# One plain chunk fewer ahead of the seven-product chunks, and one weight split held back in the queue

## The chip, the cores and the metric

The kernel runs on one core of one Trainium2 chip. The metric is device time in microseconds (us) for one execution, the median of the runs shown. Engines: PE is TensorE's matmul, PEld its weight load, DVE is VectorE, ACT is ScalarE, POOL is GpSimd, and SP is SyncE, whose queue (SPq) issues the loads. "L462" is line 462 of the kernel before.

## What is computed

A decoder trunk of two layers on 512 tokens of width 1024. Each layer is a SwiGLU feed-forward, a mixer, and a second feed-forward. All four feed-forwards have the same form, and the change touches only them:

```
h = h + 0.5 * swiglu(rmsnorm(h, g), wg, wu, wd)
def swiglu(u, wg, wu, wd):
    return (jax.nn.silu(u @ wg) * (u @ wu)) @ wd      # wg, wu: 1024 x 2816, wd: 2816 x 1024
```

The mixer of the first layer is a causal pooling, that of the second an attention over a shared latent. The final step is an RMSNorm.

## The kernel before

**Tiles and precision.** The 2816 hidden channels are 22 chunks of 128, and the model width is 8 chunks of 128; activations are held channel by token, 128 x 512. Every operand is split in two parts, hi and lo, and each product is three matmuls (`mm3`, L116 to L118): hi*hi, hi of the weights by lo of the data, lo of the weights by hi of the data. A weight unit of 128x1024 is loaded (tile `wraw`, 4 buffers), cast by ScalarE (`whi`) and its remainder taken by VectorE (`wlo`); plain units and the two wide units of a seven-product chunk share 4 buffers (`wsplit`).

**The plain chunks.** A feed-forward begins with chunks 0 and 1 (gate and up of both in four PSUM tiles, by `wfirst`), then chunk 2 (gate over all 8 channels, then up), then chunk 3 (gate and up in turn for each channel): 48 matmuls of 512 columns for a chunk. Behind the first channel of chunk 2's up part the norm's factor is spread over the partitions by two matmuls (`on_all`, L301 and L305, from `norm.spread`); its copy `rb` (ACT L307) is what every gate is multiplied by. `gated(g)` (L526 to L534) makes the middle values of a plain chunk: gate times rb (L530), silu (ACT L516), times rb again (L517), times up (L533), then cast and remainder (`split_mid`, L523 and L524: tiles `mh`, `ml`).

**The seven-product chunks.** From chunk `N_FIRST` = 4 on, gate and up of a chunk are made by a Strassen-like scheme of seven products P1 to P7 on 256 columns, of 12 matmuls each (84 for a chunk). `group_weights(g)` (L191) loads two raw units `ra` and `rb`, splits `a` (a11 and a12, for P1 and P2) and `f` (a22, for P4), has GpSimd make four sums in place (L201), and splits the sums: `s13` (for P5 and P7) behind the first two sums, `s24` (for P6 and P3) behind all four. The data side needs differences of halves: t1, t2 and t4 are made ahead, T3 (`prepare_t3`, L428 to L432 with L437) is written over the second half of the first four channels' operand, so only once the plain chunks have read it; P7 reads it. PSUM results are combined by way of copies: `c1` behind P1, `c16` behind P6, `c167` behind P7 (all ACT L462). P7 adds on to the tile that `c16` was copied from, so it waits for that copy. P4 and P3 of a chunk run during the next chunk; P3 is followed by L504, L478, silu, L517, L509, L510, `mh` and `ml`.

**Down products.** They are spread over the chunks by `down_steps(g)`: in chunk 4 the channels 0 and 1 take the middle values of chunks 0 and 1 (behind P2) and of chunk 2 (behind P5); in chunk 5, behind P2, they take those of chunk 3.

**What sets the order.** In the feed-forward PE runs in the order written. On ACT, DVE, POOL and SP a planner picks, when an engine comes free in its own model of the times, the first instruction in program order that is ready; that order is then fixed, and each engine runs it in turn. `queued_behind(steps)` adds an edge in the queue of the engine of each step, without a wait for the step's end. In the kernel before, the weights of chunk 4 and all T3 work are queued behind the last DVE step of the spread and behind the copy `rb`.

Of the kernel before, what the change touches and what calls it, by code (L numbers as in the profile page):

```python
# [16 lines left out]
P = 128  # L17
T = 512
D = 1024
ND = D // P  # L20
F = 2816
NF = F // P
HT = T // 2
N_FIRST = 4
PART = 4
N_MID = 8
H = 16
# [15 lines left out]
def down_steps(g):  # L43


    i, base = g % PART, g - g % PART - PART
    most, end, whole = range(base, base + PART - 1), [base + PART - 1], range(base, base + PART)
    if i == 0 and base == 0:
        return ([(d, most[:2], True, False) for d in range(2)], [(d, most[2:], False, False) for d in range(2)], [])
    if i == 0:  # L50
        return [], [], [(d, most, True, False) for d in range(2)]
    early = [(d, end, False, True) for d in range(2)] if i == 1 else []
    return early, [], [(d, whole, True, True) for d in (2 * i, 2 * i + 1)]
# [15 lines left out]
def trunk_kernel(  # L69
# [23 lines left out]
    nc = tc.nc  # L93
# [14 lines left out]
    def mm_tile():  # L108
        return psum.tile([P, T], F32, tag="mm", name="mm")
# [4 lines left out]
    def mm3(out, w, x, start, stop, **kw):  # L114

        nc.tensor.matmul(out, w[0], x[0], start=start, stop=False, **kw)  # L116
        nc.tensor.matmul(out, w[0], x[1], start=False, stop=False, **kw)  # L117
        nc.tensor.matmul(out, w[1], x[0], start=False, stop=stop, **kw)  # L118
# [67 lines left out]
    def split_into(tiles, raw, s):  # L186
        hi, lo = tiles
        nc.scalar.copy(hi[:, s], raw[:, s])  # L188
        nc.vector.tensor_tensor(out=lo[:, s], in0=raw[:, s], in1=f(hi[:, s]), op=ALU.subtract)  # L189

    def group_weights(idx, g, wb):  # L191

        ra, rb = (wraw_sb.tile([P, UNIT], F32, tag="wraw", name="wraw") for _ in range(2))
        nc.sync.dma_start(ra, wgu[idx, g - 2, 0])
        nc.sync.dma_start(rb, wgu[idx, g - 2, 1])
        q0, q1, whole = slice(0, 512), slice(512, UNIT), slice(0, UNIT)

        def add(out, x, y):  # L200
            nc.gpsimd.tensor_tensor(out=out, in0=x, in1=y, op=ALU.add)  # L201

        a = split_w(ra, wsplit_sb, "w")
        split_into(a, ra, whole)
        a22 = split_w(rb[:, q0], room.wf, "f")
        split_into(a22, rb[:, q0], q0)
        add(rb[:, q0], rb[:, q0], rb[:, q1])
        add(rb[:, q1], rb[:, q1], ra[:, q0])
        s13 = split_w(rb, wsplit_sb, "w")
        split_into(s13, rb, whole)  # L210
        add(ra[:, q0], rb[:, q0], ra[:, q0])
        add(ra[:, q1], ra[:, q0], ra[:, q1])
        s24 = split_w(ra, wb, "w")
        split_into(s24, ra, whole)
        a, a22, s13, s24 = part(a, 8, P), part(a22, 4, P), part(s13, 8, P), part(s24, 8, P)

        def of(w, at):
            return lambda k: [x[:, at + k] for x in w]

        return dict(a11=of(a, 0), a12=of(a, 4), a22=of(a22, 0), s1=of(s13, 0), s3=of(s13, 4), s2=of(s24, 0), s4=of(s24, 4))  # L220
# [227 lines left out]
    def ffn(idx, norm, on_h, first=None, last=None):  # L448
        with tc.tile_pool(name="mid", bufs=1) as midp, tc.tile_pool(name="wb", bufs=2) as wb, \
                tc.manual_schedule(engines={mybir.EngineType.PE}):  # L450
            weights, acc, act, mids = {}, {}, {}, {}

            def product(g, to, w, x, start=True):
                if start:
# [4 lines left out]

            def copy_of(g, name):  # L460
                t = act[g][name] = room.act.tile([P, HT], F32, tag=name, name=name)
                nc.scalar.copy(t, acc[g]["x"])  # L462
                return t

            def p1(g):
                product(g, "x", "a11", "b11")
# [70 lines left out]
            whole = slice(0, T)  # L537
# [29 lines left out]
                        norm.quarters.prepare(u)  # L567
            quarters, r, steps = norm.quarters, norm.r(), []
            ws = [part(load_w(wgu[idx, 0, m]), ND, P) for m in range(2)]
            for m in range(2):  # L570
                o = mm_tile()
                for c in range(ND):
                    mm3(o, [x[:, (c + 4 * m) % ND] for x in ws[m]], norm.gh[c], c == 0, c == ND - 1)
                    if m == 1 and c == 0:
                        rb = norm.spread(r, steps)
                        for j in range(2):
                            gated(j, ps[2 * j], ps[2 * j + 1])
                ps.append(o)
            gated(2, ps[4], ps[5])

            ws = [part(load_w(wgu[idx, 1, m]), ND, P) for m in range(2)]
            units[0] = part(load_w(wd[idx, 0]), 8, P)

            with queued_behind(steps):
                weights[N_FIRST] = group_weights(idx, N_FIRST, wb)
            ps = [mm_tile() for _ in range(2)]
            for c in range(ND):
                for m in range(2):
                    mm3(ps[m], [x[:, (c + 4 * m) % ND] for x in ws[m]], norm.gh[c], c == 0, c == ND - 1)
                if c == ND // 2 - 1:  # L590
                    with queued_behind(steps):
                        for k in range(ND // 2):
                            quarters.prepare_t3(k)
            gated(3, *ps)

            before = None
            for g in range(N_FIRST, NF):
                early, middle, late = down_steps(g)
                if g > N_FIRST:
                    weights[g] = group_weights(idx, g, wb)  # L600
                acc[g], act[g] = {}, {}
                p1(g)
                p2(g)
# [538 lines left out]
```

## Time and profile before

| | |
|---|---|
| time, median of 2 runs | 1725.56 us (1724.69 to 1726.42) |
| the profiled execution | 1728.71 us, its span 1726.9 us |
| PE busy | 1706.3 us, 99% of the span, 10816 matmuls |
| PEld, DVE, ACT, POOL busy | 1543.4, 1302.8, 850.9, 570.0 us (89, 75, 49, 33%) |
| granted TensorE clock, mean of the span | 0.995 |
| DMA | 166.77 MB, 31% of the 16 engines' time |

A busy PE is not PE at its peak, because matmuls overlap; the distance from one start to the next says more than a duration. Feed-forwards 1 to 4 have their chunk 2 at about 32, 406, 770 and 1386 us of the span.

### The profile page before, as it was taken

What the parts mean: (1) busy time and instruction counts of PE and PEld (TensorE: products, weight loads), DVE (VectorE), ACT (ScalarE), POOL (GpSimd) and SP (SyncE); (2) the same over time, 40 slices, a digit from 0 to 9 for tenths busy, and PEclk for the clock granted to TensorE, in tenths of its full rate; (3) what the DMA queues carried; (4) which work ended last, traced back from release to release, by engine and by line L of the source; (5) the groups of instructions that cost most, each with busy time, mean ns of one, the idle gap of its engine ahead of it and who ended that gap; (6) DMA issues with size and microseconds to landing.
All of it is one profiled execution on the core that took longest, in us unless ns stands there. A gap on an engine that the chain in (4) does not pass through costs nothing. (4 is left out here: it accounts for less than half of the span.)

```text
span 1726.9 us, 27436 instructions
## 1 busy us (share of the span) xinstructions
PE 1706.3 (99%) x10816; PEld 1543.4 (89%) x10816; DVE 1302.8 (75%) x2086; ACT 850.9 (49%) x1391; POOL 570.0 (33%) x388
## 2 busy tenths in 40 slices
PE   8999999999999999999999999999999999999998
PEld 6899999998899999888999999888888889999997
DVE  8877777789777777897777777787765787777775
ACT  6544444464444444454444444586655544444443
POOL 2433344133333344113334432422221234334421
PEclk9999999999999999999999999999999999999999
DMA  6233333322333322332333333332231232333331
GB/s 208 86 99 110 110 91 95 121 87 62 110 99 110 109 91 95 106 95 86 111 111 92 94 108 104 94 90 56 61 86 62 72 100 86 111 110 98 95 102 50
DMA packets 49585, 166.77 MB, mean 97 GB/s; under 512 B 6320, under 2 KB 6320, under 8 KB 49456
## 3 DMA queue, kind: packets, MB, share of 16 engines
q1 hardware_dynamic: 49312, 164.98, 31.1%
q8 instruction: 85, 1.39, 0.3%
q14 instruction: 44, 0.36, 0.1%
q10 hardware_dynamic: 144, 0.04, 0.0%
HBM read 158.44 MB, written 2.10 MB: 93 GB/s over the span
## 5 line engine op out<-in xcount | busy, mean ns | idle before, releaser
L201 POOL TENSOR_TENSOR wraw<-wraw 128x512 f32<-128x512 f32 x288 | 438.9, 1525 | 749.2 <-DVE flo L189 703.5
L116 PE MATMUL mm<-gh_hi,whi 128*128 128x256 f32 (+1 forms) x1424 | 435.2, 306 | 6.9 <-ACT c L462 6.9
L118 PE MATMUL mm<-gh_hi,wlo 128*128 128x256 f32 (+1 forms) x1424 | 435.1, 306 | 1.1 <-DVE wlo L146 1.1
L117 PE MATMUL mm<-gh_lo,whi 128*128 128x256 f32 (+1 forms) x1424 | 434.7, 305 | 0.5 <-DVE gh_lo L328 0.5
L188 ACT CAST whi<-wraw 128x1024 fp32r<-128x1024 f32 x216 | 226.9, 1053 | 207.7 <-POOL wraw L201 184.4
L116 PEld LDWEIGHTS mm<-gh_hi,whi 128*128 128x128 f32 x1424 | 274.6, 193 | 21.6 <-ACT c L462 8.6
L117 PEld LDWEIGHTS mm<-gh_lo,whi 128*128 128x128 f32 x1424 | 274.5, 193 | 14.3 <-DVE gh_lo L328 0.9
L118 PEld LDWEIGHTS mm<-gh_hi,wlo 128*128 128x128 f32 x1424 | 274.4, 193 | 13.4 <-DVE wlo L146 2.7
L189 DVE TENSOR_TENSOR wlo<-wraw,whi 128x1024 fp32r<-128x1024 f32 x216 | 271.3, 1257 | 3.1 <-ACT whi L188 3.0
L116 PE MATMUL aux<-mh,whi 128*128 128x512 f32 x576 | 225.3, 391 | 0.0
L117 PE MATMUL aux<-ml,whi 128*128 128x512 f32 x576 | 225.2, 391 | 0.0
L118 PE MATMUL aux<-mh,wlo 128*128 128x512 f32 x576 | 224.1, 389 | 0.0
L146 DVE TENSOR_TENSOR wlo<-wraw,whi 128x1024 fp32r<-128x1024 f32 (+1 forms) x158 | 184.8, 1170 | 31.0 <-ACT whi L145 30.6
L145 ACT CAST whi<-wraw 128x1024 fp32r<-128x1024 f32 (+2 forms) x188 | 162.3, 878 | 86.4 <-PE mm L117 46.7
L504 DVE TENSOR_TENSOR mm<-c,mm 128x256 f32<-128x256 f32 x72 | 30.9, 429 | 197.9 <-PE mm L118 197.9
L116 PE MATMUL mm<-t_hi,whi 128*128 128x256 f32 (+1 forms) x592 | 169.5, 286 | 0.6 <-ACT c L462 0.6
L118 PE MATMUL mm<-t_hi,wlo 128*128 128x256 f32 (+1 forms) x592 | 169.3, 286 | 0.0
L117 PE MATMUL mm<-t_lo,whi 128*128 128x256 f32 (+1 forms) x592 | 169.2, 286 | 0.0
L345 POOL TENSOR_TENSOR sq_acc<-sq_acc,sq 128x512 f32<-128x512 f32 (+1 forms) x47 | 72.5, 1543 | 203.1 <-ACT sq L341 193.4
L517 DVE TENSOR_TENSOR gate<-gate,rb 128x512 f32<-128x512 f32 x88 | 133.6, 1523 | 2.8 <-ACT gate L516 2.8
L462 ACT COPY c<-mm 128x256 f32<-128x256 f32 x216 | 79.8, 370 | 103.9 <-PE mm L118 103.9
L118 PEld LDWEIGHTS aux<-mh,wlo 128*128 128x128 f32 x576 | 108.2, 188 | 23.2
(209 smaller groups left out, 3328.2 us busy)
## 6 DMA issues: line engine op xcount, KB each, us to landing
wraw<-in_wgu SPq DMA_DIRECT2D x160, 512.0 KB, 3.7
wraw<-in_wd SPq DMA_DIRECT2D x88, 512.0 KB, 3.6
wraw<-in_wo SPq DMA_DIRECT2D x16, 512.0 KB, 3.8
wraw<-in_wfirst SPq DMA_DIRECT2D x12, 512.0 KB, 3.6
wraw<-in_wheads SPq DMA_DIRECT2D x8, 512.0 KB, 3.5
h<-in_xT SPq DMA_DIRECT2D x8, 256.0 KB, 5.4
wraw<-in_wfirst SPq DMA_DIRECT2D x8, 256.0 KB, 5.3
qr<-yh SPq DMA_DIRECT2D x32, 64.0 KB, 2.1
```

What stands on the lines that cost most here:

```text
L116: nc.tensor.matmul(out, w[0], x[0], start=start, stop=False, **kw)
L117: nc.tensor.matmul(out, w[0], x[1], start=False, stop=False, **kw)
L118: nc.tensor.matmul(out, w[1], x[0], start=False, stop=stop, **kw)
L145: nc.scalar.copy(hi[:, s], raw[:, s]).ins,
L146: lo_engines[i % len(lo_engines)].tensor_tensor(out=lo[:, s], in0=raw[:, s], in1=f(hi[:, s]), op=ALU.subtract).ins]
L188: nc.scalar.copy(hi[:, s], raw[:, s])
L189: nc.vector.tensor_tensor(out=lo[:, s], in0=raw[:, s], in1=f(hi[:, s]), op=ALU.subtract)
L201: nc.gpsimd.tensor_tensor(out=out, in0=x, in1=y, op=ALU.add)
L345: nc.gpsimd.tensor_tensor(out=self.acc[:, ts], in0=self.acc[:, ts], in1=self.sq[:, ts], op=ALU.add)
L462: nc.scalar.copy(t, acc[g]["x"])
L504: nc.vector.tensor_tensor(out=y, in0=act[g]["c16"], in1=y, op=ALU.add)
L517: nc.vector.tensor_tensor(out=gate, in0=gate, in1=rb, op=ALU.mult)
```

## The change

One constant goes from 4 to 3, so the plain chunks are 0, 1 and 2, and chunk 3 is the first of the seven-product chunks. Chunk 2 is now multiplied by channel (gate and up in turn, as chunk 3 was). The spread of the norm's factor and `gated` of chunks 0 and 1 stand behind its fifth channel, and behind them, in one block queued behind the spread and the copy `rb`, the weights of chunk 3 and all T3 work. The load of the first down unit ahead of the loop is gone: `down` loads it when it first needs it, in chunk 4. From chunk 4 on, the split of `s24` (on ScalarE, and with it VectorE's remainder) is queued behind the copy `c16` of the chunk in front. `down_steps` returns nothing for chunk 3; the steps of the other chunks are the same.

```diff
-N_FIRST = 4
+N_FIRST = 3
...
     i, base = g % PART, g - g % PART - PART
+    if base < 0:
+        return [], [], []
...
-    def group_weights(idx, g, wb):
+    def group_weights(idx, g, wb, last_behind=()):
...
         s24 = split_w(ra, wb, "w")
-        split_into(s24, ra, whole)
+        with queued_behind(last_behind):
+            split_into(s24, ra, whole)
...
-                nc.scalar.copy(t, acc[g]["x"])
-                return t
+                copied[g, name] = nc.scalar.copy(t, acc[g]["x"]).ins
...
             ws = [part(load_w(wgu[idx, 0, m]), ND, P) for m in range(2)]
-            for m in range(2):
-                o = mm_tile()
-                for c in range(ND):
-                    mm3(o, [x[:, (c + 4 * m) % ND] for x in ws[m]], norm.gh[c], c == 0, c == ND - 1)
-                    if m == 1 and c == 0:
-                        rb = norm.spread(r, steps)
-                        for j in range(2):
-                            gated(j, ps[2 * j], ps[2 * j + 1])
-                ps.append(o)
-            gated(2, ps[4], ps[5])
-
-            ws = [part(load_w(wgu[idx, 1, m]), ND, P) for m in range(2)]
-            units[0] = part(load_w(wd[idx, 0]), 8, P)
-
-            with queued_behind(steps):
-                weights[N_FIRST] = group_weights(idx, N_FIRST, wb)
-            ps = [mm_tile() for _ in range(2)]
+
+            os = [mm_tile() for _ in range(2)]
             for c in range(ND):
                 for m in range(2):
-                    mm3(ps[m], [x[:, (c + 4 * m) % ND] for x in ws[m]], norm.gh[c], c == 0, c == ND - 1)
-                if c == ND // 2 - 1:
+                    mm3(os[m], [x[:, (c + 4 * m) % ND] for x in ws[m]], norm.gh[c], c == 0, c == ND - 1)
+                if c == ND // 2:
+                    rb = norm.spread(r, steps)
+                    for j in range(2):
+                        gated(j, ps[2 * j], ps[2 * j + 1])
+
                     with queued_behind(steps):
+                        weights[N_FIRST] = group_weights(idx, N_FIRST, wb)
                         for k in range(ND // 2):
                             quarters.prepare_t3(k)
-            gated(3, *ps)
+            gated(2, *os)
...
-                    weights[g] = group_weights(idx, g, wb)
+                    weights[g] = group_weights(idx, g, wb, [copied[before, "c16"]])
```

## Rows read from the trace of the kernel before

**Rows 1.** Page, busy us of each engine (share of the span) and instructions.
```profile
PE 1706.3 (99%) x10816; PEld 1543.4 (89%) x10816; DVE 1302.8 (75%) x2086; ACT 850.9 (49%) x1391; POOL 570.0 (33%) x388
```
**Rows 2.** Timeline, PE, feed-forward 2: start us, duration us, instruction, idle before and releaser.
```profile
413.28 0.39 PE L116 MATMUL mm<-gh_hi,whi 128*128 128x512 f32 x1
...
428.95 0.28 PE L116 MATMUL mm<-gh_hi,whi 128*128 128x256 f32 x1
...
431.82 0.40 PE L116 MATMUL aux<-mh,whi 128*128 128x512 f32 x1
```
**Rows 3.** Timeline, PE: waits from chunk 2 on, feed-forwards 1 to 4.
```profile
39.94 0.47 PE L301 MATMUL aux<-diag,ones_r 128*128 128x512 f32 x1 [1.56 <-DVE diag L294]
41.10 0.50 PE L305 MATMUL aux<-diag,ones_r 128*128 128x512 f32 x1 [0.69 <-DVE diag L303]
69.26 0.39 PE L116 MATMUL mm<-gh_hi,whi 128*128 128x256 f32 x1 [0.49 <-ACT c L462]
412.95 0.50 PE L305 MATMUL aux<-diag,ones_r 128*128 128x512 f32 x1 [0.39 <-DVE diag L303]
441.10 0.58 PE L116 MATMUL mm<-gh_hi,whi 128*128 128x256 f32 x1 [2.10 <-ACT c L462]
798.34 0.39 PE L116 MATMUL mm<-t_hi,whi 128*128 128x256 f32 x1 [0.60 <-ACT c L462]
805.01 0.39 PE L116 MATMUL mm<-gh_hi,whi 128*128 128x256 f32 x1 [2.14 <-ACT c L462]
1420.66 0.56 PE L116 MATMUL mm<-gh_hi,whi 128*128 128x256 f32 x1 [2.14 <-ACT c L462]
```
**Rows 4.** Windows: us, busy (x) PE PEld DVE ACT POOL, PEclk, DMA share, GB/s.
```profile
41.70:45.00 3.30, 3.30 (x9) 2.53 (x8) 3.23 (x6) 3.30 (x7) 0.19 (x1) 0.51 0.51 138
441.10:444.40 3.30, 3.30 (x15) 3.30 (x16) 0.93 (x1) 0.50 (x1) 0.00 (x0) 0.50 0.50 139
806.70:809.80 3.10, 3.10 (x16) 3.10 (x16) 1.56 (x2) 1.63 (x3) 0.00 (x0) 0.51 0.53 169
1420.70:1423.80 3.10, 3.10 (x15) 3.10 (x16) 0.90 (x1) 0.37 (x1) 0.00 (x0) 0.50 0.46 137
```
**Rows 5.** Timeline, ACT, ahead of the wait at 441.10.
```profile
439.73 1.04 ACT L188 CAST whi<-wraw 128x1024 fp32r<-128x1024 f32 x1 [1.82 <-POOL wraw L201]
440.68 0.36 ACT L462 COPY c<-mm 128x256 f32<-128x256 f32 x1
```
**Rows 6.** Timeline, ACT, DVE and POOL: the first weights behind the spread; four sums.
```profile
413.48 0.59 ACT L307 COPY rb<-aux 128x512 f32<-128x512 f32 x1 [0.92 <-PE aux L305]
413.97 0.62 ACT L188 CAST fhi<-wraw 128x512 fp32r<-128x512 f32 x1
...
415.91 0.68 DVE L189 TENSOR_TENSOR flo<-wraw,fhi 128x512 fp32r<-128x512 f32 x1
...
78.00 6.28 POOL L201 TENSOR_TENSOR wraw<-wraw 128x512 f32<-128x512 f32 x4 [10.15 <-DVE flo L189]
```
**Rows 7.** Page, costliest groups: xcount | busy us, mean ns | idle before.
```profile
L188 ACT CAST whi<-wraw 128x1024 fp32r<-128x1024 f32 x216 | 226.9, 1053 | 207.7 <-POOL wraw L201 184.4
...
L189 DVE TENSOR_TENSOR wlo<-wraw,whi 128x1024 fp32r<-128x1024 f32 x216 | 271.3, 1257 | 3.1 <-ACT whi L188 3.0
```
**Rows 8.** Windows, from the spread to P1 of chunk 4, feed-forward 2.
```profile
412.17:428.95 16.78, 16.39 (x72) 13.25 (x71) 16.70 (x21) 9.44 (x18) 9.15 (x6) 1.00 0.13 39
```
**Rows 9.** Timeline, DVE: an instruction beside GpSimd's sums.
```profile
418.34 1.78 DVE L517 TENSOR_TENSOR gate<-gate,rb 128x512 f32<-128x512 f32 x1
```
**Rows 10.** Timeline, PE and DVE: P3 of chunk 4 and what follows it.
```profile
79.38 0.28 PE L116 MATMUL mm<-gh_hi,whi 128*128 128x256 f32 x1
...
81.02 0.43 DVE L504 TENSOR_TENSOR mm<-c,mm 128x256 f32<-128x256 f32 x1 [3.10 <-PE mm L118]
...
88.63 0.67 DVE L524 TENSOR_TENSOR ml<-m,mh 128x512 fp32r<-128x512 f32 x1
```
**Rows 11.** Timeline, ACT: the copy `rb` of feed-forward 3.
```profile
759.10 0.58 ACT L307 COPY rb<-aux 128x512 f32<-128x512 f32 x1
```

More of the change, by code (lines that the diff above doesn't have):

```diff
@@ L450, in ffn @@
                 tc.manual_schedule(engines={mybir.EngineType.PE}):
-            weights, acc, act, mids = {}, {}, {}, {}
+            weights, acc, act, mids, copied = {}, {}, {}, {}, {}
             def product(g, to, w, x, start=True):
```

## The prediction

> **What bounds the kernel now.** I read the page's busy times first, then the waits of PE, then the timelines around each wait. PE is busy 99% of the span, VectorE 75% [rows 1], so the question is what the order of PE's work costs and where PE waits. In the plain chunks a 512-column matmul starts every (428.95 - 413.28) / 69 = 0.2271 us; in P1 and P2 a 256-column one every (431.82 - 428.95) / 24 = 0.1196 us [rows 2]. From chunk 2 on, the four feed-forwards have only eight waits of PE worth naming [rows 3]: three at the spread of the norm's factor (1.56, 0.69, 0.39 us) and five behind a copy of ScalarE (0.49, 2.10, 0.60, 2.14, 2.14 us), all in the first pair of seven-product chunks. About the four longest the granted clock stands at 0.50 to 0.51 for 3.1 to 3.3 us [rows 4]: 1.2 GHz in place of 2.4, a loss of 1.5 to 1.65 us each, 6.3 us together. The cause of the 2.1 us waits is an order in ScalarE's queue: the cast of the next chunk's `s24` waits 1.82 us for GpSimd's sums, and the copy `c16`, which P7 needs, stands behind it [rows 5].
>
> **What the change takes away.** Arithmetic: a plain chunk is 48 x 0.2271 = 10.90 us, a seven-product chunk 84 x 0.1196 = 10.05 us, so 0.85 us less in each feed-forward, 3.4 in all [rows 2]. The Trainium skill (TensorE: Matmul & The Clock Gate, Back-to-back issue gap) gives 518 and 262 cycles warm, 215.8 and 109.2 ns; by it the four chunks would give back 4.7 us. Both measured starts are slower than that, the small one by more, and I keep 3.4.
>
> The copy: with the split of `s24` queued behind the `c16` of the chunk in front, the order of [rows 5] can't occur. I take away all five copy waits, 0.49 + 2.10 + 0.60 + 2.14 + 2.14 = 7.5 us [rows 3], and the three low-clock stretches behind them, 4.7 us [rows 4]. In later chunks PE waits for nothing, so the edge can win nothing there.
>
> The spread: two weight splits (old chunk 3) leave VectorE's queue ahead of the norm's factor, and PE has 30 matmuls ahead of the spread, not 27. I take away 2.25 us and 1.6 of low clock in feed-forward 1, and 0.4 in feed-forward 2 [rows 3, 4]. All taken away: 3.4 + 7.5 + 4.7 + 2.25 + 1.6 + 0.4 = 19.9 us.
>
> **What it adds: a first chunk without cover.** All of chunk 3's weights, and T3, are queued behind the copy `rb`. P6 needs `s24`, at the end of a chain that passes through four engines. In the rows of feed-forward 2 [rows 6]: second spread matmul 412.95, copy until 414.07, cast of `f` from 413.97, its remainder done at 416.59, four sums in 6.28 us (the steady stretch at 78.00), cast 1.05, remainder 1.26 [rows 7]: 425.2, or 12.2 us behind the spread. PE will ask for that remainder after 0.33 + 18 x 0.2271 + 24 x 0.1196 + 2 x 0.1196 = 7.5 us. Before, a whole plain chunk and six down steps more lay in between. So PE waits 4.7 us. Lower bound: the remainder of `f` follows its cast at once (415.27), 3.4 us. Upper bound: from the spread to P1 of chunk 4 VectorE was busy 16.70 of 16.78 us [rows 8]; if P7 of chunk 3 has to wait for as much work, and for two remainders of 1.26 more, that is 19.2 us against 10.9, a wait of 8.3 us for the first chunk as a whole. I take 6.0, nearer to the chain, because its rows are an ordered sequence, while part of VectorE's 16.70 is not needed by then. An idle of that length brought a half-clock stretch in every case of [rows 3, 4], so 1.6 more: 7.6 us. It holds in feed-forwards 1, 2 and 4: 22.8 us (bounds 15.0 and 29.7).
>
> The price of the sums for VectorE is seen in one row: a 128x512 instruction of 0.68 us takes 1.78 us beside them [rows 6, 9], so about 1.1 us for each sum. The Trainium skill (SBUF — State Buffer, section "SBUF: two separate sides") goes further: GpSimd and a VectorE instruction with two SBUF inputs take a shared port pair by exclusive lock, and the later one blocks for the whole instruction. That would be up to 1.57 us a sum, and 4 x 0.47 x 3 = 5.6 us on the upper bound.
>
> **And a late chunk 3.** The down steps of chunk 5, behind its P2, need chunk 3's `mh` and `ml`. Those were plain values, finished early; now they come behind P3 of chunk 3, which runs in chunk 4. In the trace P3 of chunk 4 ends at 79.38 + 12 x 0.1196 = 80.82, and its `ml` at 89.30 [rows 10]: 8.5 us. There, two more down channels stand in front of the next use; here only P7, P1 and P2 do, 36 x 0.1196 = 4.3 us. Upper bound 4.2 us and a half-clock stretch, 5.8; lower bound 0, since the eight instructions of the tail alone, without what VectorE slips in, come to about that room. I take 2.5, with the clock at half its price, 3.3 us, nearer to the measured tail than to the bare one. All four feed-forwards: 13.2 us (0 to 23.2).
>
> Feed-forward 3 escapes the first of these: its `rb` is copied at 759.10 [rows 11], eleven us ahead of its chunk 2, so the sums are done in time.
>
> Costed at nothing: the first down unit's load moves behind the raw units of chunk 4 on SP's queue and waits for a buffer that chunk 3's `s13` frees; seven products (10 us) cover it, and without them its cast and remainder (2.3 us) and the load would show. The loads of chunk 3 are as many bytes in the same places. Four more sums in POOL's queue, three and a half splits for two, and chunk 3's tail for one `gated` lie on engines with room later on; where they have none is priced above.
>
> **Sum.** 22.8 + 13.2 - 19.9 = +16.1 us. Against the profiled execution, 1728.7 (its span is 1726.9), that is 1744.8; this execution lies 3.2 us above the median, 1725.56, so for the median 1741.7 us, slower by 0.9%. Two per cent, 34.5 us, is about what a measurement of this kernel tells from no change; the limits are 1691 and 1760.
>
> **Rivals.**
> 1. *VectorE keeps up* (not slower). Place: its queue behind the spread and behind P3. With two splits gone from in front, `f`'s remainder goes at once, and the tail is not interleaved: 15.0 + 0 - 19.9 = -4.9, 1721 us. It decides from the point where the added waits fall under 19.9 us. For it: the idle stretches of VectorE behind the old waits. Against: [rows 8]. Chance 0.22.
> 2. *VectorE is the bound* of the first two seven-product chunks, with GpSimd's sums beside its work: both upper bounds, 29.7 + 23.2 - 19.9 = +33, 1759 us. For it: [rows 8, 9]; against: the planner runs chunk 4's first sums early, which are not queued behind the spread. With the whole-instruction lock of the SBUF page the time would be 1764. Chance 0.18.
> 3. *The edge does nothing*: another cast that waits stands ahead of `c16`, and the 12.2 us stay: 1754 us. For it: the wait at 798.34 is for another copy. Chance 0.05.
>
> **How the numbers follow.** The forecast has 0.55 and 1741.5 us. The range, 1720 to 1760, goes from rival 1 to rival 2. Over 2% slower is half of rival 2 and a little of the forecast: 0.1. Over 2% faster would need more than all that can be taken away: 0.01. Within: 0.89.
>
> **What would show it.** P6 of chunk 3 waiting 4 to 8 us in feed-forwards 1, 2, 4 and not in 3, behind ScalarE's cast or VectorE's remainder; the down steps of chunk 5 waiting for L524 or L523; no 2.1 us wait on L462; a clock of 0.5 behind each long wait; the spread of feed-forward 1 without its 2.25 us. I am wrong if P6 of chunk 3 starts within 2 us, or if the old copy waits remain.

## The result and the profile after

The changed kernel takes **1801.24 us** (median of 2 runs, 1800.86 to 1801.62) against 1725.56: a ratio of 1.0441, 95% interval 1.0415 to 1.0466. It is slower by 4.4%, where the forecast said 0.9% and the range ended at 1760. The profiled execution has a span of 1799.8 us, against 1726.9.

PE has almost the same work and more idle time. The page of the changed kernel, busy us and share of the span, against [rows 1]:

```profile
PE 1717.7 (95%) x10960; PEld 1559.8 (87%) x10960; DVE 1321.5 (73%) x2114; ACT 859.4 (48%) x1411; POOL 588.6 (33%) x404
```

The waits of PE in the changed kernel (timeline), against [rows 3]. Line numbers are two to four higher than before.

```profile
38.73 0.39 PE L305 MATMUL aux<-diag,ones_r 128*128 128x512 f32 x1
...
57.59 0.58 PE L118 MATMUL mm<-t_hi,whi 128*128 128x256 f32 x1 [11.12 <-ACT whi L190]
64.26 0.58 PE L120 MATMUL mm<-t_hi,wlo 128*128 128x256 f32 x1 [5.88 <-DVE wlo L191]
...
451.79 0.58 PE L118 MATMUL mm<-t_hi,whi 128*128 128x256 f32 x1 [11.15 <-ACT whi L190]
458.47 0.58 PE L120 MATMUL mm<-t_hi,wlo 128*128 128x256 f32 x1 [5.88 <-DVE wlo L191]
486.74 0.80 PE L118 MATMUL aux<-mh,whi 128*128 128x512 f32 x1 [4.25 <-ACT mh L526]
...
816.73 0.76 PE L118 MATMUL mm<-gh_hi,whi 128*128 128x512 f32 x1 [3.89 <-DVE gate L533]
859.49 0.49 PE L118 MATMUL aux<-mh,whi 128*128 128x512 f32 x1 [4.30 <-ACT mh L526]
```

Three kinds of wait are to be seen. P6 of chunk 3 waits for its cast and again for its remainder, 17.0 us in feed-forwards 1, 2 and 4 (FF1, FF2, FF4). The down steps of chunk 5 wait 4.25 to 4.30 us for chunk 3's `mh` in all four. And in FF3 chunk 2 waits 3.89 us for an accumulator. What the forecast took away is gone: the spread of FF1 (38.73) has no wait, and no 2.1 us stands on the copy.

Counted from start to start against the spacings of [rows 2], and up to the first matmul of chunk 4's P1, the first kind loses 19.8, 20.5 and 20.4 us in FF1, 2 and 4. The second then loses 6.6, 7.0, 6.7 and 7.0 us, 27.3 together, and the third 7.0 us: 95.0 us in all. (An expectation below has 7.2, 8.5, 6.7 and 8.4 us for the second kind, 30.8 together; the difference is the end of the first kind's low clock.) The feed-forwards of the kernel before lose about 20 us by this count from their chunk 2 on. The net of 75 us, less the 3.4 us of the arithmetic, is some 72; the spans differ by 72.9.

Two windows of the changed kernel (columns as in [rows 4]): the first from the end of VectorE's wait for `rb` to where chunk 3's last remainder is done, the second the stretch at low clock.

```profile
434.35:458.42 24.07, 7.09 (x42) 6.01 (x40) 24.07 (x27) 13.71 (x23) 11.66 (x8) 0.70 0.09 24
444.00:464.00 20.00, 6.33 (x28) 6.04 (x29) 18.05 (x21) 7.74 (x12) 5.83 (x5) 0.50 0.34 103
```

VectorE is busy 24.07 of 24.07 us: [rows 8] over again, nearly half as long again. PE, idle for most of it, is at a granted clock of 0.50, 1.2 GHz, for 20 us. What stands in VectorE's queue, in the timeline of the changed kernel, with GpSimd's sums beside it:

```profile
437.45 2.91 POOL L204 TENSOR_TENSOR wraw<-wraw 128x512 f32<-128x512 f32 x2 [13.53 <-DVE flo L191]
439.73 1.18 DVE L191 TENSOR_TENSOR flo<-wraw,fhi 128x512 fp32r<-128x512 f32 x1
440.84 2.35 DVE L520 TENSOR_TENSOR gate<-gate,rb 128x512 f32<-128x512 f32 x2
441.00 6.12 POOL L204 TENSOR_TENSOR wraw<-wraw 128x512 f32<-128x512 f32 x4 [0.63 <-DVE flo L191]
443.12 2.88 DVE L441 TENSOR_TENSOR gh_lo<-b,gh_hi 128x256 fp32r<-128x256 f32 x2
445.92 1.75 DVE L520 TENSOR_TENSOR gate<-gate,rb 128x512 f32<-128x512 f32 x1
449.75 1.99 ACT L190 CAST whi<-wraw 128x1024 fp32r<-128x1024 f32 x2
453.79 2.35 DVE L527 TENSOR_TENSOR ml<-m,mh 128x512 fp32r<-128x512 f32 x2
456.07 2.35 DVE L191 TENSOR_TENSOR wlo<-wraw,whi 128x1024 fp32r<-128x1024 f32 x2
```

GpSimd makes two sums of chunk 3, then waits for chunk 4's `flo` and mixes chunk 4's sums with the rest; the pairs of casts and remainders at 449.75 and 456.07 are chunk 4's `s13` first, chunk 3's `s24` second. The kernel without the edge (below), whose tiles are named by chunk, shows the same pair, D for chunk 4 and C for chunk 3:

```profile
455.79 1.21 DVE L191 TENSOR_TENSOR sbDl<-rbD,sbDh 128x1024 fp32r<-128x1024 f32 x1
456.93 1.21 DVE L191 TENSOR_TENSOR saCl<-raC,saCh 128x1024 fp32r<-128x1024 f32 x1
```

So chunk 4's work, not held behind anything, goes ahead of what PE waits for.

### The profile page after: what moved, and what is told of

Read it like the earlier page. It is cut to its first block, busy times and chain, and to the rows that moved or that the text cites. A ratio compares the mean times of both kernels' runs of the same rounds, so it can differ in the third digit from the quotient of the medians.

```text
span 1799.8 us, 27783 instructions
## 1 busy us (share of the span) xinstructions
PE 1717.7 (95%) x10960; PEld 1559.8 (87%) x10960; DVE 1321.5 (73%) x2114; ACT 859.4 (48%) x1411; POOL 588.6 (33%) x404
## 4 chain that ended last, share of the span: by engine, by line
PE 90%; DVE 6%; issue 1%; DMA 1%; ACT 1%; SPq 0%; DVEq 0%; ACTq 0%
PE mm L118 21%; PE mm L120 21%; PE mm L119 21%; PE aux L119 7%; PE aux L118 7%; PE aux L120 7%; DVE wlo L191 1%; PE mm L883 1%; PE aux L920 1%; DVE b L435 1%; DVE wlo L148 1%; DVE gate L520 1%; PE mm L895 1%; PE mm L885 1%; PE mm L884 1%
## 5 line engine op out<-in xcount | busy, mean ns | idle before, releaser
L204 POOL TENSOR_TENSOR wraw<-wraw 128x512 f32<-128x512 f32 x304 | 458.0, 1508 | 803.3 <-DVE flo L191 732.2
L120 PE MATMUL mm<-gh_hi,wlo 128*128 128x256 f32 (+1 forms) x1424 | 426.5, 299 | 0.8 <-DVE wlo L148 0.8
L190 ACT CAST whi<-wraw 128x1024 fp32r<-128x1024 f32 x228 | 239.1, 1052 | 211.3 <-POOL wraw L204 181.4
L191 DVE TENSOR_TENSOR wlo<-wraw,whi 128x1024 fp32r<-128x1024 f32 x228 | 283.3, 1243 | 27.9 <-ACT whi L190 27.9
L118 PE MATMUL mm<-t_hi,whi 128*128 128x256 f32 (+1 forms) x624 | 182.1, 292 | 33.6 <-ACT whi L190 33.4
L120 PE MATMUL mm<-t_hi,wlo 128*128 128x256 f32 (+1 forms) x624 | 181.8, 291 | 17.6 <-DVE wlo L191 17.6
L148 DVE TENSOR_TENSOR wlo<-wraw,whi 128x1024 fp32r<-128x1024 f32 (+1 forms) x150 | 172.3, 1149 | 24.1 <-ACT whi L147 23.7
L119 PE MATMUL mm<-t_lo,whi 128*128 128x256 f32 (+1 forms) x624 | 181.3, 291 | 0.0
L118 PEld LDWEIGHTS mm<-t_hi,whi 128*128 128x128 f32 x624 | 122.9, 197 | 35.0 <-ACT whi L190 34.0
L118 PEld LDWEIGHTS aux<-mh,whi 128*128 128x128 f32 x576 | 109.3, 190 | 37.9 <-ACT mh L526 17.9
```

The lines of the kernel that those rows point to most:

```text
L148: lo_engines[i % len(lo_engines)].tensor_tensor(out=lo[:, s], in0=raw[:, s], in1=f(hi[:, s]), op=ALU.subtract).ins]
```

## The experiments

In the kernels below the tiles are renamed by chunk, and nothing else by that: `raC`, `sbCh`, `saCl` belong to chunk 3 (`sb` is `s13`, `sa` is `s24`), those with D to chunk 4, `mhA`, `mhB`, `mhK`, `mhC` to chunks 0 to 3. Each ratio is to the kernel before, run beside that kernel, with its 95% interval; the kernel before had medians of 1724.7 to 1726.4 us there, so differences of a microsecond or two between kernels of different sections say nothing. The edits are shown in part.

### The edge alone

```diff
 # kernel before, N_FIRST = 4
-        split_into(s24, ra, whole)
+        with queued_behind(last_behind):        # the c16 of the chunk in front
+            split_into(s24, ra, whole)
```

> The kernel before with only the new edge: four chunks plain as before, but the last split of a chunk's weights (both halves of s24) queued behind the copy of P6 of the chunk in front. My account of the kernel before gave 7.5 us to the five waits of P5 on that copy, and 4.7 us to the low granted clock behind three of them. Theory (the waits are on the path and nothing takes their place): 1725.6 - 12.2, about 1713 us, and no wait of about 2.1 us on the copy of ScalarE is left. Rival (the split comes later and its own reader then waits as long): 1724 to 1727 us, and a wait of P6 on whi or wlo stands where the copy wait stood.

Measured: 1715.22 us against 1724.68 for the kernel before, 0.9944 (0.9932 to 0.9957), 9.5 us less. Timeline of ScalarE and PE at the place of [rows 5]:

```profile
436.20 0.37 ACT L466 COPY c<-mm 128x256 f32<-128x256 f32 x1
437.26 0.28 PE L116 MATMUL mm<-gh_hi,sbDh 128*128 128x256 f32 x1
438.13 1.05 ACT L188 CAST saEh<-raE 128x1024 fp32r<-128x1024 f32 x1 [1.57 <-POOL raE L204]
```

The cast that waits for GpSimd now stands behind the copy, and P7 starts without a wait. (The expectation writes P5; four of the five waits were P7's, and that of 0.60 us was P6's, on the copy `c1`.) Of the four copy waits over 0.5 us none is left; the largest is 0.27. The theory holds; its 12.2 us lie just above the interval's 7.4 to 11.7. This kernel is faster than both others.

### Three chunks without the edge

```diff
-  weights[g] = group_weights(idx, g, wb, [copied[before, "c16"]])
+  weights[g] = group_weights(idx, g, wb)
```

> The changed kernel without the edge: three chunks plain, the third by channel, but the split of s24 free to go ahead of the copy. In the changed kernel's own order the edge moves one cast in each of the four feed-forwards, that of chunk 4's s24. Theory (P6 of chunk 3 waits 17 us for weights in FF1, 2 and 4, so a copy wait of 2 us behind it only moves): 1798 to 1806 us against 1801.2. Rival (the edge is worth what the copy waits cost in the kernel before, whatever stands in front): 1810 to 1816 us, with waits of about 2.1 us on the copy.

Measured: 1801.35 us, 1.0445 (1.0431 to 1.0459). The edge is worth nothing in the changed kernel: P6 waits 11.16 and 5.88 us in FF2, and no copy wait over 0.3 us comes back. In FF2 the cast of chunk 4's `s24` is done at 455.91, and the copy `c16` is due only at 460.74. In FF3, where P6 does not wait, the old order is there: the cast waits 1.02 us for GpSimd in front of the copy, but P7 waits only 0.15 us for it. The 12.2 us that the forecast took off for the edge would have gone without it.

### The down steps of chunk 5 later

```diff
+    if base == 0:          # i == 1: chunk 5; early is empty elsewhere
+        return [], early, [(d, whole, True, True) for d in (2 * i, 2 * i + 1)]
     return early, [], [(d, whole, True, True) for d in (2 * i, 2 * i + 1)]
```

> The changed kernel, but the first two down steps of chunk 5, which need chunk 3's mid, stand behind P5 of chunk 5 instead of behind its P2. In the changed kernel PE waits there 4.25 to 4.30 us for chunk 3's mid in each of the four feed-forwards, and the low granted clock behind it brings the loss to 7.2, 8.5, 6.7 and 8.4 us by the spacing of its matmuls. Theory (chunk 3 is just late by less than P4, P6 and P5 take, and nothing else is late): the four waits go, 30.8 us less, 1770 us; with a second wait of 1 us each at the place where they were, 1775. Rival (VectorE is the bound there, and whatever reads its work next waits as long): 1797 to 1803 us, with waits on other tiles of VectorE of 3 to 4 us in each feed-forward.

Measured: 1780.67 us, 1.0326 (1.0312 to 1.034): 20.6 us less than the changed kernel, three quarters of the 27.3 us of the count above, and between theory and rival. The wait for `mh` is gone; PE now waits for the remainder alone, 1.34 or 1.35 us in all four, in FF2:

```profile
484.52 0.50 PE L121 MATMUL aux<-mlC,whi 128*128 128x512 f32 x1 [1.35 <-DVE mlC L535]
```

Chunk 3 is late by little more than P4, P6 and P5 take, and the loss is separate from P6's. That rival is out.

### Chunk 3's weights not queued behind the spread

```diff
-  with queued_behind(steps):
-      weights[N_FIRST] = group_weights(idx, N_FIRST, wb)
+  weights[N_FIRST] = group_weights(idx, N_FIRST, wb)
+  with queued_behind(steps):
       for k in range(ND // 2):
```

> The changed kernel, but the weights of chunk 3 (their sums on GpSimd, casts on ScalarE, remainders on VectorE) are no longer queued behind the spread of the norm; the T3 sums and differences of the quarters still are. Nothing is left out. Theory (P6 of chunk 3 waits because its weights start only at the spread, and in queues where chunk 4's come ahead): the waits of 11.15 and 5.88 us in FF1, 2 and 4 go, with their low clock 18.9 us each; about 50 to 57 us less, 1745 to 1752 us. A smaller gain by half (one of the two waits stays): 1772. Rival (VectorE has more work in this stretch than the stretch is long, so the order doesn't matter): 1786 to 1801 us, with P6 of chunk 3 or the first reader of another of its tiles waiting 10 us or more.

Measured: 1793.13 us, 1.0396 (1.038 to 1.0412), 8 us less. P6 waits no more, but PE in FF2 stops ahead of it and behind it:

```profile
439.76 0.79 PE L308 MATMUL aux<-diag,ones_r 128*128 128x512 f32 x1 [5.70 <-DVE diag L301]
459.09 0.58 PE L118 MATMUL mm<-gh_hi,sbCh 128*128 128x256 f32 x1 [5.13 <-ACT c L469]
```

The splits are now in front of the norm's factor in VectorE's queue, and P7 waits. The time is what the rival said; the single waits are of 5 to 7 us, not its 10, and there are two of them. That was the first sign that the work, and not its place, is too much.

### Chunk 4 behind, the tails behind, the factor

Three steps, each on top of the one before: chunk 4's weights behind the last of chunk 3's sums; the tails of chunks 0 to 2 (`m`, `mh`, `ml`) behind chunk 3's last remainder; chunk 3's weights behind the end of the factor in place of the copy `rb`.

```diff
+  behind=done[:1] if g == N_FIRST + 1 else ()   # chunk 4: last sum of chunk 3
...
+  with queued_behind(done[1:]):                 # chunk 3's last remainder
+      for tail in tails:
+          tail()
...
-  with queued_behind(steps):                    # diag and rb
+  with queued_behind(steps[:1]):                # diag alone
       weights[N_FIRST] = group_weights(idx, N_FIRST, wb, done=done)
```

> The changed kernel, but the weights of chunk 4 are queued behind the last of chunk 3's four sums on GpSimd: in the built order GpSimd now makes chunk 3's four sums first, ScalarE casts chunk 3's s24 before chunk 4's s13, VectorE takes their remainders in the same order. Nothing is left out. In the changed kernel P6 of chunk 3 waits 11.15 and 5.88 us in FF1, 2 and 4. Theory A (chunk 4's sums in front are the whole delay, so that my chain of 12.2 us holds without them): the two waits together fall to about 6 us, 11 us less in three feed-forwards, 1768 us. Theory B (the chain passes in-order queues of three engines, and chunk 3's last cast still stands behind the first mid's cast on ScalarE, its remainder behind the products m and the first ml on VectorE): only the second wait shortens, 1 to 5 us less in three feed-forwards, 1786 to 1798 us.

> As the kernel with chunk 4's weights behind chunk 3's sums, and in addition the tails of the three plain chunks (the product m, its cast mh and remainder ml) are queued behind the last remainder of chunk 3's weights. Nothing is left out. Theory B (the queues' order): chunk 3's last cast and remainder now follow their sums within about 3 us, so the two waits of P6 fall from 11.15 and 5.88 us to about 4 and 1; with less low clock behind them 11 to 14 us less in three feed-forwards, 1759 to 1768 us. Theory C (VectorE has more work up to P1 of chunk 4 than the stretch is long, in any order): what P6 gains comes back at the next reader of VectorE's work, the copies of P7 or the down steps of chunk 4 that need the three mids, with waits of 5 us or more there, and the time is 1785 us or more.

> As the kernel with the tails later, and in addition chunk 3's weights are queued behind the end of the norm's factor on VectorE instead of behind the copy of its spread on ScalarE; T3 stays behind the copy. In FF2 of the changed kernel the factor is done at 430.71 and the copy starts at 433.73, with ScalarE idle 8.16 us and VectorE 3.64 us ahead of their next instruction. Nothing is left out. Theory B: the whole chain starts 3.0 to 3.5 us earlier, P6 of chunk 3 waits 0 to 2 us, and the time is 1743 to 1757 us. Theory C: no gain over the kernel with the tails later, since the work ahead of P1 of chunk 4 is the same; the wait goes to the copy rb or the next reader of VectorE.

Measured: 1792.80 us (1.0389, 1.0371 to 1.0406), 1784.01 (1.0339, 1.0324 to 1.0355) and 1783.45 (1.0334, 1.0319 to 1.035). The first has the time of theory B, though the cast's wait shortened (9.28) and not the remainder's (6.01). The second is 17 us under the changed kernel, half of what B said, with waits of 7.96 and 4.94 us; its time is close to theory C's 1785, but none of C's new waits is there. The third, the kernel with the factor, gave nothing, as theory C said. PE in FF2 of the third:

```profile
439.37 0.43 PE L118 MATMUL mm<-t_hi,saCh 128*128 128x256 f32 x1 [3.00 <-ACT c L475]
443.72 0.58 PE L120 MATMUL mm<-t_hi,saCl 128*128 128x256 f32 x1 [3.71 <-DVE saCl L191]
451.24 0.58 PE L118 MATMUL mm<-gh_hi,sbCh 128*128 128x256 f32 x1 [2.46 <-ACT c L475]
```

Three waits of 9.2 us stand in place of two of 12.9, and the time is the same. In FF2 the clock stays low for longer, and that takes back what the waits give: from 452 to 456, about as far behind the spread in both, it is 0.93 in the second (first row) and 0.50 in the third.

```profile
452.00:456.00 4.00, 4.00 (x34) 4.00 (x33) 4.00 (x7) 2.23 (x3) 0.00 (x0) 0.93 0.49 166
452.00:456.00 4.00, 4.00 (x21) 4.00 (x20) 2.16 (x2) 1.45 (x3) 0.00 (x0) 0.50 0.50 157
```

### Chunk 4 held back altogether

```diff
-  behind=done[:1] if g == N_FIRST + 1 else ()
+  behind=done[1:] if g == N_FIRST + 1 else ()   # chunk 3's last remainder
```

> As the kernel whose chunk 3 weights are queued behind the factor (1783.5 us), but chunk 4's weights are queued behind the last remainder of chunk 3's weights on VectorE, not behind chunk 3's sums on GpSimd: VectorE has two fewer remainders ahead of chunk 3's last one, and GpSimd makes chunk 4's sums after it. Nothing is left out. In that kernel, FF2, VectorE is busy from 432 to 444 without a break, chunk 3's last remainder takes 2.28 us beside chunk 4's sums (1.21 alone) and ends 3.71 us after P6 has its cast. Theory C (VectorE is the bound of the stretch, and work that P6 doesn't need costs its own length there): the remainder ends 2 to 3 us earlier, the wait of 3.71 falls to 1 to 1.5, and three feed-forwards give 8 to 18 us with the low clock: 1765 to 1776 us. Rival (only the order on ScalarE counts; chunk 4's work is done meanwhile and comes due later): 1780 to 1788 us, with a new wait of 2 us or more at P1 or P2 of chunk 4.

Measured: 1784.96 us, 1.0333 (1.0314 to 1.0353), no gain. PE in FF2:

```profile
438.62 0.39 PE L118 MATMUL mm<-t_hi,saCh 128*128 128x256 f32 x1 [1.65 <-ACT c L475]
440.30 0.39 PE L120 MATMUL mm<-t_hi,saCl 128*128 128x256 f32 x1 [1.17 <-DVE saCl L191]
451.73 0.58 PE L118 MATMUL mm<-gh_hi,sbCh 128*128 128x256 f32 x1 [7.41 <-ACT c L475]
```

P6's remainder comes 4 us earlier, its wait falls to 1.17 us as theory C said, and P7 pays all of it. The time is the rival's, but neither had the place: the new wait is at P7 of chunk 3. The wait named for the copy is one for T3: `c16` takes a buffer that T3's `b12` held (both have the tag `c16`, with two buffers), and ahead of the copy ScalarE stood idle 2.37 us for the third of T3's four `gh_lo`, which VectorE ends 0.3 us ahead of the last one. The window of this kernel from `rb` to there:

```profile
430.68:451.55 20.87, 10.82 (x64) 9.54 (x62) 20.87 (x27) 11.92 (x21) 9.64 (x7) 0.84 0.16 50
```

VectorE is again busy all the time.

### Chunk 3's sums on VectorE

```diff
-  nc.gpsimd.tensor_tensor(out=out, in0=x, in1=y, op=ALU.add)
+  (nc.vector if g == N_FIRST else nc.gpsimd).tensor_tensor(out=out, in0=x, in1=y, op=ALU.add)
```

> As the kernel that holds chunk 4's weights, but the four sums of chunk 3's weights are made on VectorE and not on GpSimd; GpSimd does nothing between the factor and chunk 3's last remainder. Nothing is left out. Theory C with contention (VectorE's instructions are slowed beside GpSimd's sums: two 128x512 products of gate and factor took 3.48 us beside them, 1.29 without): VectorE gets four sums of 0.6 to 0.7 us, 2.6 us in all, and loses some 5 us of slowing, so its last remainder ends about 2 us earlier than in the kernel that holds chunk 4's weights, and it is faster than that by 5 to 12 us. Rival (GpSimd's sums are in truth free for VectorE, and its rows are long for another reason): VectorE's queue becomes 2.6 us longer and the time is 5 to 10 us above that kernel, with the two products still at 3 us.

Measured: 1778.45 us, 1.0298 (1.0282 to 1.0314), 6.5 us less than with chunk 4 held: giving VectorE four more instructions made it finish sooner. Two products of gate and `rb` that took 2.38 us together there (first row) take 0.68 each here (second and third row):

```profile
433.72 2.38 DVE L529 TENSOR_TENSOR gate<-gate,rb 128x512 f32<-128x512 f32 x2
433.66 0.68 DVE L529 TENSOR_TENSOR gate<-gate,rb 128x512 f32<-128x512 f32 x1
434.86 0.68 DVE L529 TENSOR_TENSOR gate<-gate,rb 128x512 f32<-128x512 f32 x1
```

Contention with GpSimd is part of the bound. (Each of chunk 3's sums also takes 0.69 us on VectorE, against 1.3 to 1.5 on GpSimd; how the 6.5 us divide between the two was not measured.) FF3 gains by it too: the wait of its chunk 2 falls from 3.68 to 1.97 us.

### T3 first, with and without the later down steps

```diff
+  done.append(quarters.last)                     # T3's last remainder
   with queued_behind(done[1:]):                  # the tails
...
+  sums_behind=done[2:] if g == N_FIRST + 1 else ()   # chunk 4's sums
```

> As the kernel that makes chunk 3's sums on VectorE (1778.5 us), but the tails of the three plain chunks and chunk 4's four sums on GpSimd are queued behind the last remainder of T3, which P7 of chunk 3 reads. Nothing is left out. In that kernel P6 waits 1.58 us and P7 7.88 us in FF2, for the copy c16, which stands behind T3's last remainders; VectorE is busy all the time from the spread to there, and its instructions between chunk 3's last remainder and T3's last one are two tails, two remainders of chunk 4, and two instructions slowed to 2.88 and 1.43 us beside chunk 4's sums. Theory C (it is VectorE's whole work up to P7, so only taking work out of the stretch helps): T3's last remainder ends about 5 us earlier, P7 waits 2 to 3 us; a new wait of 1 to 3 us at P6 of chunk 4 for its later sums takes some back; 1757 to 1768 us. Rival (P7 waits for something else, a buffer or ScalarE's order): no change of P7's wait, 1775 to 1785 us.

> As the kernel with T3 first, and the first two down steps of chunk 5 behind P5, as in the run that moved only them. Nothing is left out. Theory (the two losses, a first chunk without cover and a late chunk 3, are separate): the gain of 20.6 us measured for the move alone is had again, 1736 to 1748 us. Rival (both are one backlog of VectorE, and what the first repair leaves undone comes due here): less than 10 us of gain, 1752 us or more. That it gets below the kernel before (1725.6 us) or the one with the edge alone (1715 us) neither theory expects.

Measured: 1768.77 us (1.0251, 1.0234 to 1.0267), and with the down steps moved 1749.85 (1.014, 1.012 to 1.016). The first is 9.7 us less than with chunk 3's sums on VectorE, 1 us above theory C's range; the move then gives 18.9 us, nearly what it gave alone, and the time is 2 us above its theory's range. The two losses are separate. VectorE, GpSimd and PE in FF2 of the second:

```profile
421.45 0.88 DVE L448 SCALAR_TENSOR_TENSOR b<-h,g_sb,b 128x256 f32<-128x256 f32 x2
425.78 0.75 DVE L454 TENSOR_TENSOR gh_lo<-b,gh_hi 128x256 fp32r<-128x256 f32 x2
...
430.26 2.89 DVE L448 SCALAR_TENSOR_TENSOR b<-h,g_sb,b 128x256 f32<-128x256 f32 x2
431.55 1.32 POOL L209 TENSOR_TENSOR rbD<-rbD,raD 128x512 f32<-128x512 f32 x1
432.95 1.32 POOL L209 TENSOR_TENSOR raD<-rbD,raD 128x512 f32<-128x512 f32 x1
433.08 2.90 DVE L454 TENSOR_TENSOR gh_lo<-b,gh_hi 128x256 fp32r<-128x256 f32 x2
435.07 0.58 PE L120 MATMUL mm<-gh_hi,sbCh 128*128 128x256 f32 x1 [4.13 <-ACT c L479]
```

Chunk 4's sums ran beside T3, from 429.87 on, although they were to be queued behind T3's last remainder, which ends at 435.98: `queued_behind` orders the queue of the step's own engine, here VectorE's, and does not make GpSimd wait for it. The same two pairs take 1.63 us without the sums and 5.79 with them; the 4.16 us between are about the 4.13 us that P7 waits.

### The sums away from T3

```diff
-  split_into(a22, rb[:, q0], q0)
+  with queued_behind(sums_behind):
+      split_into(a22, rb[:, q0], q0)             # the sums wait for its remainder
```

> As the kernel with T3 first and the down steps moved (1749.9 us), but the split of chunk 4's a22 block (f), whose remainder the first of chunk 4's sums has to wait for, is queued behind T3's last remainder as well, so that GpSimd can't make those sums beside T3. Nothing is left out. In that kernel the sums began right behind f's remainder, at 429.87 in FF2, and beside them T3's two scaled differences took 2.89 us and its two remainders 2.90, against 0.88 and 0.75 for the same pairs without GpSimd earlier in the same feed-forward; P7 waits 4.13 us. Theory (VectorE loses about 4.2 us there to GpSimd's sums): both pairs fall to 0.9 us or less and P7's wait to under 1 us, in FF2 and FF4 and by 2 us in FF1; the sums come due later, at P6 of chunk 4, which may wait 1 to 4 us for them; the time is between 1732 (no new wait) and 1750 us (all of it taken back there). Rival (the long rows are waits for ScalarE's casts of T3, and GpSimd is a bystander): the pairs stay at 2.9 us and P7's wait at 4 us, with the time at or above 1750.

Measured: 1755.21 us, 1.0174 (1.0157 to 1.019), about 5 us more. VectorE and PE in FF2:

```profile
433.74 0.88 DVE L449 SCALAR_TENSOR_TENSOR b<-h,g_sb,b 128x256 f32<-128x256 f32 x2
434.70 0.82 DVE L455 TENSOR_TENSOR gh_lo<-b,gh_hi 128x256 fp32r<-128x256 f32 x2
443.11 0.79 PE L120 MATMUL aux<-mhA,whi 128*128 128x512 f32 x1 [2.27 <-ACT whi L149]
446.67 0.79 PE L122 MATMUL aux<-mhA,wlo 128*128 128x512 f32 x1 [2.34 <-DVE wlo L150]
```

The mechanism is as the theory has it: both pairs are short and P7 no longer waits (0.60 us in FF4). The time is not: the new wait is not at P6 of chunk 4 but at the down unit, whose cast and remainder now stand behind chunk 4's late `s13`. The debt moved on once more.

### Chunk 2 of FF3

Two runs were meant for the 3.89 us in FF3. One multiplies chunk 2 one accumulator after the other. The other takes channels 0 to 3 into the first accumulator, then the same four into the second, and the rest in turn; the edit is that of the second.

```diff
+  first = [(c, m) for m in range(2) for c in range(ND // 2)]
-  for c in range(ND):
-      for m in range(2):
+  for c, m in first + [(c, m) for c in range(ND // 2, ND) for m in range(2)]:
```

> The changed kernel, but chunk 2 is multiplied one accumulator after the other (gate, then up) instead of channel by channel into both; the spread stays behind the same number of matmuls of it, 30. Nothing is left out. In FF3 of the changed kernel the first matmul of chunk 2 into its second accumulator waits 3.89 us for VectorE's reading of another one (the gate of a chunk in front), and the stretch loses 7.0 us with its low granted clock. Theory (two accumulators are needed at once where only one is free): that wait goes and nothing else changes, 1794 us. Rival (the second accumulator is needed 24 matmuls, 5.4 us, later, but the tile is freed by a chain that is late anyway): 1798 to 1802 us, with the wait at the 25th matmul.

> The changed kernel, but chunk 2 multiplies its channels 0 to 3 into the first accumulator, then the same four into the second, and only channels 4 to 7 in turn into both; the spread stays behind 30 matmuls. The second accumulator is so needed 9 matmuls later than in the changed kernel, 2.0 us at 0.2271. Nothing is left out. In FF3 of the changed kernel its first matmul waits 3.89 us for VectorE's reading of an older accumulator and the stretch loses 7.0 us with its low granted clock. Theory: the wait falls to 1.9 us, the time by 2.0 us, and by up to 4 us if the low clock shortens too: 1797 to 1799.5 us. Rival (the wait is a chain that follows PE, not a fixed time): no change, 1801 us and 3.9 us of wait.

The first took 1825.63 us (1.0578, 1.0562 to 1.0594), and says nothing on the question. Unlike what its expectation says, it changes the computation: T3 overwrites halves of channels 0 to 3, which its second accumulator then reads, and PE waits 18.85 us for T3 in FF2. The second took 1801.61 us (1.0433, 1.0416 to 1.0449). PE in FF3:

```profile
816.91 0.47 PE L118 MATMUL mm<-gh_hi,whi 128*128 128x512 f32 x1 [1.81 <-DVE gate L539]
832.69 0.39 PE L118 MATMUL mm<-t_hi,saCh 128*128 128x256 f32 x1 [2.87 <-ACT c L469]
```

The wait shrank by 2.1 us, as the theory said, and P6 then waits 2.87 us where it had waited for nothing over 0.5. The time is the rival's. The copy that P6 waits for stands in ScalarE's queue behind casts, and ScalarE had itself been idle 5.45 us for VectorE's `gh_lo`; that VectorE's queue is the bound in FF3 too is likely by that, and not shown.

### The row of repairs

How long after the first matmul of the spread P6's first remainder and P7's first matmul start in FF2 (differences of the starts in the timelines). Without a wait it would be 7.6 and 10.3 us by [rows 2].

| kernel | P6's remainder | P7 | time, ratio |
|---|---|---|---|
| the changed kernel | 25.4 | 30.2 | 1801.2, 1.0441 |
| chunk 4 behind the sums | 23.7 | 28.3 | 1792.8, 1.0389 |
| and the tails | 21.3 | 25.3 | 1784.0, 1.0339 |
| and the factor | 14.9 | 22.4 | 1783.5, 1.0334 |
| and chunk 4 held | 10.9 | 22.3 | 1785.0, 1.0333 |
| and the sums on VectorE | 9.7 | 20.4 | 1778.5, 1.0298 |
| and T3 first | 9.7 | 16.7 | 1768.8, 1.0251 |
| and the down steps later | 9.7 | 16.7 | 1749.9, 1.0140 |
| and the sums away from T3 | 9.7 | 13.9 | 1755.2, 1.0174 |

From the third line to the fifth P6's column falls by 10.4 us, P7's by 3.0 and the time not at all. P7's 3.0 us go to the low clock: 200 matmuls into chunk 4 both kernels are 60.4 us behind the spread. From there on the time falls with P7's column and with the moved down steps, until the last line, where the next wait is behind P7.

## Why the prediction was wrong

**Right.** P6 of chunk 3 waits in FF1, 2 and 4 and not in FF3, behind the cast and then the remainder; the down steps of chunk 5 wait for `mh` and `ml` in all four; the spread of FF1 has no wait; the waits on `c16` are gone; the clock is at 0.50 behind each long wait. Every place but the one in FF3 was named. The sizes failed, while the forecast adds up rightly what it takes from the rows. (Of the six down steps that it puts in front of P6 in the kernel before, only four are there; two stand behind P5. No number hangs on it.)

**The step that failed most** is the choice in the first chunk without cover: "I take 6.0, nearer to the chain, because its rows are an ordered sequence, while part of VectorE's 16.70 is not needed by then." In the order that was built, what isn't needed by then is in front all the same: 26 VectorE instructions run without a break from `rb` to the end of chunk 3's last remainder, and the tails of the plain chunks and three remainders of chunk 4 are among them. With the tails and chunk 4 behind it, and its start moved to the factor, that remainder is used 10.9 us after the spread in place of 25.4. The measured loss is 20 us, not 7.6, three times: 38 us of the miss of 59.5. The upper bound of 8.3 failed too: it has 19.2 us of work from the spread up to P7, while VectorE of the changed kernel ends chunk 3's last remainder alone 25.3 us behind the spread (458.42 against 433.08), with T3's last remainders still to come. More of it is chunk 4's, and more of it is slowed: the three rows above of 2.35, 2.88 and 1.75 us, five instructions, take about 1.3, 0.76 and 0.68 in kernels without sums beside them, so 4.2 us of the 24.1 are slowing there alone.

**Rival 2** had the mechanism, VectorE as the bound with GpSimd's sums beside it, at 0.18, and its 1759 us were still 42 us short. Its "against", that "the planner runs chunk 4's first sums early, which are not queued behind the spread", was the wrong way round. The sums ran no earlier than the spread and went in between chunk 3's; queueing them behind took 8.4 us off. That the two added losses are separate terms was right: the moved down steps gave 20.6 us alone and 18.9 on top of the repairs.

**The late chunk 3** was taken at 3.3 us a feed-forward, 13.2 in all, with 23.2 as the end of the range. It lost 27.3, 14 us of the miss, and moving two steps gave back 20.6. The wait of 4.25 us is the upper bound's 4.2: the tail was as long as [rows 10] have it, and not shorter. The clock behind it cost 2.3 to 2.8 us and not the 0.8 that "half its price" put there.

**FF3** was said to escape. It escapes P6's wait, but loses 7.0 us, the rest of the miss, at a place that the forecast doesn't name: multiplying by channel needs two free accumulators at once, and there only one was free.

**Taken away.** The edge was taken at 12.2 us; alone it gives 9.5, beside three chunks nothing. Behind P6's wait of 17 us the copy is due so late that the cast is long done (FF2 above); in FF3 the sums come early enough.

**Costed at nothing** was the down unit, with the note that without its cover its cast and remainder would show. The last repair took the cover away, and they show: 2.27 and 2.34 us.

What stays open is whether any order of these three chunks beats the edge alone. The best of the row is at 1.0140, the edge alone at 0.9944; no run makes chunk 4's sums elsewhere than on GpSimd; and how much of VectorE's 24.1 us is slowing was measured for some rows, not for all of its instructions.

## What to carry to other kernels

Where an engine is busy for the whole of a stretch, add up its queue to the first instruction that PE can't do without, in the order in which it stands, with everything that isn't needed yet; a dependency chain is only a lower bound. A repair that takes one wait away is worth something when the next reader of the same engine starts earlier too, so follow two readers and not one. And try the small part of a change alone: the edge by itself won 9.5 us, where the whole lost 75.7.

## What the runs showed of the hardware

A VectorE instruction on two SBUF operands is held up beside GpSimd's sums, by most of a sum: a 128x256 pair of 0.88 us took 2.89 us beside sums of 1.32 to 1.60 us, 1.0 us more for each of the two. In the kernel before, the products of gate and `rb` that no sum overlaps take 0.68 us (median of 16), those beside a sum 1.78 (median of 72), and none over 1.79. One that reads an accumulator is not held up: in the kernel with the factor, VectorE and GpSimd in FF2,

```profile
433.36 3.48 DVE L529 TENSOR_TENSOR gate<-gate,rb 128x512 f32<-128x512 f32 x2
436.38 1.59 POOL L207 TENSOR_TENSOR rbD<-rbD,raD 128x512 f32<-128x512 f32 x1
436.77 0.68 DVE L547 TENSOR_TENSOR gate<-mm,rb 128x512 f32<-128x512 f32 x1
```

the product of an accumulator and `rb` keeps its 0.68 us beside a sum, where the two products of SBUF tiles just ahead of it took 1.74 on average. The Trainium skill (SBUF — State Buffer, section "SBUF: two separate sides") says that the two share a port pair by an exclusive lock for the whole instruction, and names for VectorE an instruction with two SBUF inputs or in a two-port mode. These rows agree: two SBUF inputs are held up, by no more than a sum's length, and one SBUF input beside an accumulator is not; no run here shows the two-port mode.

The other thing not expected was the price of several short waits: 9.2 us of them cost as much as 12.9 us in two. In FF2 the clock was at 0.50 until 456 in place of 452.
